# A decoder layer with retrieved experts: transposes of a listed block in one run, full-width products, later factors, earlier gathers, four selection batches

## The chip, the cores and the metric

The kernel runs on one core of a Trainium2 chip. The core has a matrix engine (PE, TensorE; its weight loads are shown apart as PEld), three engines for elementwise work (DVE or VectorE, ACT or ScalarE, POOL or GpSimd), a queue engine (SP) that issues plain transfers, and 16 DMA engines. Each engine takes its instructions in the order of the program; semaphores order the engines against each other. The metric is the time on the device, in microseconds (us), as the median of several runs; lower is better.

## The reference

One layer on 256 tokens of width 2048, in float32: attention with two kinds of heads, then a feed-forward part that looks up single-neuron experts, then a gated embedding, each with a residual and a layer norm. The change lies in the feed-forward part:

```
q  = (x @ wq) as 8 heads of 256, split into halves a and b of 128
sa, sb = a @ keys0.T, b @ keys1.T            # 128 scores each
va, ia = top_k(sa, 16);  vb, ib = top_k(sb, 16)
top, sel = top_k(va[:, None] + vb[None, :], 16)   # of 256 sums
expert = (ia * 128 + ib)[sel];  gate = softmax(top)
act = gelu(u[expert] . x)                    # u: 16384 x 2048
out = sum over the 8 * 16 experts of gate * act * v[expert]
```

So each token asks for 128 of 16384 rows of u, and for the same rows of v.

## The kernel before, in words

**Tokens in groups.** The first 32 tokens (NSP) are served one by one: 32 gathers (NSLOT) of 128 rows of u, and 32 of v, each of 128 x 2048 floats; DVE multiplies and adds what they bring (`sparse_work`, L1245; `use`, L1265). The other 224 tokens are seven groups of 32. An expert that any of them wants is *listed* in one of 43 classes by the set of groups that want it: one group, a pair, a line of three, a quad of four, or the rest. Each class has a fixed capacity, and the lists are cut into 101 blocks of 128 experts (`Block`, L85; `_blocks`, L101): 42 blocks of one group, 21 of two, 14 of three, 14 of four, 10 of all seven. `U_ORDER` (L152) is the order of the blocks in the u stage: four quads, then a mixture of quads, lines and strips of pairs, then the rest, then the singles. `V_ORDER` is that of the v stage.

**The stages around the change.**

1. *Queries and selection* (L1310 to L1334). Sixteen half-head queries run on PE (`query`, L761); ACT copies them out, PE makes the scores, and ACT copies these. DVE finds the best 16 per half (`best_scores`) and, for a batch of heads, the best pairs and their indices (`best_pairs`, L792). `BATCH` (L48) says after which query which heads are taken.
2. *Counting* (`flags`, L910). For each token DVE makes two one-hot matrices, and PE sums their products by group. In every fifth batch of eight tokens ACT makes one of the two (`act_one_hot`). `classes` (L940) turns counts into class masks, `offsets` and `running` (L998) into places in the lists; all 13 calls of `running` come before the first list.
3. *The u stage* (L1522 to L1546), the main loop. Per block, POOL issues an indirect gather of 128 rows of u (`fetch_u`, five slots). The rows are needed with the model dimension on the partitions, so PE turns them, four 128x128 transposes at a time into one PSUM bank (`turn`, L1387), and ACT copies that to `uT`. Then PE multiplies (`u_products`, L1399): the 32 tokens of a group are the stationary operand, 32 columns of the array wide, and the turned rows stream through, 128 columns; up to four groups, or four parts of one group's sum, stand side by side in the array. Transposes and products of a quarter of the block alternate, four times per block. The result has tokens on the partitions, so ACT copies it (`part`), and PE turns it back and adds the parts (`u_out`, L1424; tile `ps_A`). ACT applies gelu; where the gates stand in `W` already, DVE multiplies them in at once (L1456).
4. *Side work.* Between the quarters `side(block.cost)` lets work out in small steps, `RATE` steps per microsecond of a block's cost: the further lists (`lists`), the softmax of the gates (`gates`), the places of the experts (`list_work`, `places_of`; PE sums the positions in `ps_pos`), then the weights (`place_work`, L1116: `find` on PE, `pick` on DVE, `product` and `scale` into `W`). `gathers(block.cost * GRATE)` likewise lets out the gathers of the first 32 tokens, once the lists or the gates are through. All of it is issued with `keep`, so each engine takes it in the order written: a POOL gather stands between two row fetches, a DVE sum between two steps of side work.
5. *The v stage* (from L1551) gathers the rows of v, streams them through PE against `W`, and finishes the first 32 tokens; gathers that are still owed run here (L1586). The gated embedding and the last norm follow.

**PSUM in the u stage** has eight banks: T and U two each (transposes, products), G two (lists, ranks, `ps_find`, `ps_gT`), A one, X one (`ps_pos`, then `ps_W`).

Of the kernel before, what the change touches and what calls it, by code (L numbers as in the profile page):

```python
# [10 lines left out]
F32 = mybir.dt.float32  # L11
# [36 lines left out]
BATCH = ((0, 1), (1, 1), (2, 2), (4, 2), (6, 1), (7, 1))  # L48
NGB = 3
GSCALE = 2.0 ** 15  # L50
FB = 8
FBC = 8
# [31 lines left out]

class Block:  # L85

    def __init__(self, col, pieces):
# [10 lines left out]
        self.cost = 0.44 + 0.27 * sum({"four": 4, "two": 2, "one": 1}[w] for w, _ in self.windows)  # L98
# [53 lines left out]
U_ORDER = (BLOCKS["quad"][:4] + _mix(BLOCKS["quad"][4:], BLOCKS["line"], BLOCKS["strip"])  # L152
# [8 lines left out]
RATE, GRATE, GV = 0.75, 0.12, 0.6  # L161
# [90 lines left out]
def build(tc, a, out):  # L252
# [342 lines left out]
    XF = xfp.tile([P, ND, T], F32, name="XF")  # L595
# [196 lines left out]
    def best_pairs(h0, n):  # L792
# [4 lines left out]
        cand = tkl.tile([P, 4, NCAND], F32, name="cand", tag="cand", bufs=1)  # L797
# [12 lines left out]
        s4, s2 = (tkl.tile([P, 64], U32, name=nm)[:, :nk] for nm in ("by16", "by4"))  # L810
        pF, u1 = (tkl.tile([P, 64], F32, name=nm)[:, :nk] for nm in ("pF", "u1"))
        at = [tkl.tile([P, 64, 2], F16, name=f"at{which}")[:, :nk] for which in range(2)]
# [16 lines left out]
        for which, dst in ((0, iaN), (1, ibN)):  # L829
            eq = tkl.tile([P, 64, TOPK], F16, name="eqsel", tag="eqsel", bufs=1)[:, :nk]  # L830
# [24 lines left out]
    def gates():  # L855
# [21 lines left out]
        ps = pbank(pu, "ps_gT", "G", 2)  # L877
# [32 lines left out]
    def flags(flp):  # L910
# [11 lines left out]

        for i, t0 in enumerate(range(NSP, T, FB)):
            oa, ob = (flp.tile([P, FB, P], F16, name=nm, tag=nm, bufs=3) for nm in ("oa", "ob"))
            equal(oa, io128, iaT[:, t0:t0 + FB])
            if i % 5 == 2:
                for j in range(FB):
                    act_one_hot(ob[:, j], flp, ibF[:, t0 + j:t0 + j + 1])
            else:
                equal(ob, io128, ibT[:, t0:t0 + FB])  # L930
            made.append((t0, oa, ob))
            if len(made) > 1:
                counts()
# [64 lines left out]
    def running(k0, n, tag, on_act):  # L998

        ps = pbank(pu, "ps_run", tag, 2)  # L1000
# [60 lines left out]
    def places_of(k0, n, psp):  # L1061
# [19 lines left out]
        if psp is None:  # L1081
            keep(nc.vector.tensor_tensor(posf, posf, pk[:, 0], op=ALU.add))
            return
        for j in range(n):
            keep(nc.tensor.matmul(psp, ident, pk[:, j], start=k0 + j == 0,
                                  stop=k0 + j == KR - 1))
# [5 lines left out]
    def list_work():  # L1092

        yield from lists(UPOS[id(BLOCKS["rest"][0])])
        psp = pbank(pu, "ps_pos", "X", 1)[:, :P]
        for lo, hi in ((K1, K2), (K2, K3), (K3, K4), (K4, KR)):
            for k0, n in spread(lo, hi):
                yield from places_of(k0, n, psp)
        yield
        keep(nc.vector.tensor_copy(posf, psp))  # L1100
# [6 lines left out]
        yield from places_of(KR, 1, None)  # L1107
# [8 lines left out]
    def place_work(plp):  # L1116
# [62 lines left out]
        def product(t0, ohb, hi, lo):  # L1179
            ps = pbank(pu, "ps_W", "X", 1)  # L1180
# [197 lines left out]
    rows, turned = {}, []  # L1378
# [8 lines left out]
    def turn(k):  # L1387
        i, c = divmod(k, 4)
        if i >= NB:
            return  # L1390
        ps = pbank(pu, "ps_T", "T", 2)
# [3 lines left out]
        uT = ulp.tile([P, 512], F32, name="uT", tag="uT", bufs=4)  # L1395
        keep(nc.scalar.copy(uT, ps))  # L1396
        turned.append(uT)

    def u_products(block, c, ps, uT):  # L1399
        for w, (kind, units) in enumerate(block.windows):  # L1400
            for j in range(4):
                d = 4 * c + j
                for i, u in enumerate(units):
                    q = {"four": i, "two": 2 * i + j % 2, "one": j}[kind]
                    first = d == {"four": 0, "two": j % 2, "one": j}[kind]
                    final = d == {"four": ND - 1, "two": ND - 2 + j % 2, "one": ND - 4 + j}[kind]
                    t0 = 32 * block.units[u]
                    keep(nc.tensor.matmul(  # L1408
                        ps[32 * q:32 * q + 32, w * P:(w + 1) * P], XF[:, d, t0:t0 + 32],
                        uT[:, j * P:(j + 1) * P], start=first and not w,  # L1410
                        stop=final and w == len(block.windows) - 1))
# [11 lines left out]

    def u_out(block, part):  # L1424

        A = pbank(pu, "ps_A", "A", 1)
        col = 0
        for w, (kind, units) in enumerate(block.windows):
            x = part[:, w * P:(w + 1) * P]
            n = 32 * len(units)  # L1430
            if kind == "four":
                keep(nc.tensor.transpose(A[:, col:col + n], x, ident))
            else:
                keep(nc.tensor.matmul(A[:, col:col + n], x,
                                      stack[:, 32:96] if kind == "two" else stack[:, :32],
                                      start=True, stop=True))
            col += n
# [85 lines left out]
    for _ in range(LEAD):  # L1523
        fetch_u()
# [567 lines left out]
```

## Time and profile before

| | us |
|---|---|
| median of three runs (1668.9 to 1669.56) | 1669.44 |
| the profiled execution | 1684.18 |
| its span, first to last instruction | 1682.3 |
| mean granted TensorE clock | 0.951 |
| idle PE between 629 and 1270, of 641 | 32 |
| POOL waiting for PE to free a row slot (`uf`) | 359.8 |
| ACT waiting for PE's transposes (`uT`) | 241.7 |

The rows of the page read: line of the kernel, engine, operation, out<-in with shapes, count | busy time in us, mean ns of one | idle time of the engine just before them and what ended most of it. "128*32" before a shape is the part of the array that a matmul uses, rows by columns. A float32 matmul shows as two records, a transpose as one. Durations of PE's matmuls overlap, because the engine is pipelined; the distance from one start to the next is the safer reading. In a timeline the columns are start, length, engine, line, operation, tiles and count, and in brackets the idle time before and its releaser; "issue" means that nothing that the profile shows was waited for.

### The profile page before, as it was taken

To read this page: it belongs to the slowest core of one execution; us is meant where nothing else is said; L and a number is where in the kernel's file an instruction comes from. 1 tells how busy PE (TensorE), PEld (TensorE's weight loads), DVE (VectorE), ACT (ScalarE), POOL (GpSimd) and SP (SyncE) were. 2 spreads that over 40 slices of the span, in tenths; PEclk is the share of its full clock that TensorE was granted. 3 is DMA by queue.
4 is the path that set the end of the run, shared out by engine and by line. 5 is a ranking of instruction groups with operands and counts; after the bars stand their busy time and mean duration, and the time that the engine had idled before them with its cause. 6 is when DMAs were issued, how large, how long until landed. Compare 5 with 4: busy or idle time off the path is not lost. (4 is left out here: it accounts for less than half of the span.)

```text
span 1682.3 us, 39824 instructions
## 1 busy us (share of the span) xinstructions
PE 1533.0 (91%) x16701; PEld 1099.2 (65%) x16701; DVE 885.8 (53%) x2489; ACT 674.4 (40%) x1351; POOL 418.5 (25%) x386
## 2 busy tenths in 40 slices
PE   9999999999996559999999989899999979985698
PEld 7888888878885447777776777665667312220486
DVE  5555488864678764546465555555222220022676
ACT  5587458754110535434444322255661000011452
POOL 0133023202100212233323211132343553233000
PEclk9999999999998569999999999899999999996799
DMA  8655754585440016667877746588998999889671
GB/s 288 200 162 154 237 163 147 154 307 179 158 135 1 27 52 240 232 220 260 319 281 265 267 178 211 173 310 295 375 366 319 421 420 419 345 314 421 257 266 51
DMA packets 74617, 403.27 MB, mean 240 GB/s; under 512 B 10836, under 2 KB 12916, under 8 KB 36436
## 3 DMA queue, kind: packets, MB, share of 16 engines
q0 software_dynamic: 39280, 272.11, 42.8%
q1 hardware_dynamic: 33424, 125.41, 22.4%
q10 hardware_dynamic: 1728, 3.15, 0.5%
q8 instruction: 132, 2.16, 0.5%
q14 instruction: 53, 0.43, 0.1%
HBM read 404.97 MB, written 4.45 MB: 243 GB/s over the span
## 5 line engine op out<-in xcount | busy, mean ns | idle before, releaser
L1396 ACT COPY uT<-ps_T 128x512 f32<-128x512 f32 x404 | 235.8, 587 | 254.8 <-PE ps_T L1393 241.7
L1408 PE MATMUL ps_u<-uT,XF 128*32 128x128 f32 x8064 | 316.9, 281 | 2.3 <-issue 2.1
L213 DVE TENSOR_TENSOR wl<-wf,wh 128x1024 fp32r<-128x1024 f32 (+1 forms) x199 | 212.6, 1092 | 111.0 <-ACT wh L212 109.5
L1393 PE MATMUL ps_T<-ident,uf 128*128 128x128 f32 x1616 | 261.3, 285 | 8.2 <-DMA uf<-u_rows,idx 6.4
L1408 PEld LDWEIGHTS ps_u<-uT,XF 128*32 128x32 f32 x8064 | 202.1, 110 | 76.9 <-issue 75.8
L212 ACT CAST wh<-wf 128x1024 fp32r<-128x1024 f32 (+1 forms) x199 | 172.1, 892 | 122.9 <-PE ps_v L312 34.2
L1369 POOL DMA_INDIRECT uf<-u_rows,idx x101 | 116.3, 1151 | 421.7 <-PE ps_T L1393 359.8
L1393 PEld LDWEIGHTS ps_T<-ident,uf 128*128 128x128 f32 x1616 | 176.8, 145 | 51.7 <-issue 34.7
L1564 PE MATMUL ps_v<-vf,W 128*32 128x512 f32 x1296 | 161.9, 642 | 39.0 <-DMA vf<-v_rows,idx 38.7
L291 PE MATMUL ps_qk<-X,wh 128*128 128x512 f32 x512 | 185.2, 401 | 0.0
L1564 PEld LDWEIGHTS ps_v<-vf,W 128*32 128x32 f32 x1296 | 49.3, 113 | 148.6 <-DMA vf<-v_rows,idx 78.6
L293 PE MATMUL ps_qk<-X,wl 128*128 128x256 f32 x512 | 145.7, 285 | 0.0
L1275 DVE SCALAR_TENSOR_TENSOR y<-gb,ew,y 128x2048 f32<-128x2048 f32 x31 | 72.8, 2348 | 87.1 <-DMA gb<-v_rows,eig 87.0
L303 PE MATMUL ps_q<-XF,wf 128*128 128x256 f32 x512 | 113.5, 379 | 0.0
L291 PEld LDWEIGHTS ps_qk<-X,wh 128*128 128x128 f32 x512 | 96.4, 188 | 22.0 <-issue 1.0
L1369 POOL DMA_INDIRECT vf<-v_rows,idx x73 | 76.9, 1053 | 132.1 <-PE ps_v L1564 99.2
L1456 DVE TENSOR_TENSOR W<-W,acts 128x32 f32<-128x32 f32 (+2 forms) x86 | 13.6, 188 | 171.6 <-ACT acts L1442 167.5
L303 PEld LDWEIGHTS ps_q<-XF,wf 128*128 128x128 f32 x512 | 95.9, 190 | 12.3
L293 PEld LDWEIGHTS ps_qk<-X,wl 128*128 128x128 f32 x512 | 96.3, 188 | 2.5 <-issue 1.3
L1564 PE MATMUL ps_v<-vx,W 128*32 128x512 f32 x720 | 83.1, 612 | 7.5 <-DMA vx<-v_rows,idx 6.8
L1147 DVE SCALAR_TENSOR_TENSOR junk<-io,ibF,ps_find 128x128 f16<-128x128 f16 x224 | 63.5, 344 | 38.1 <-PE ps_T L1393 20.1
L1644 ACT COPY em<-ps_emb 128x512 f32<-128x512 f32 x2 | 1.2, 585 | 196.9 <-PE ps_emb L1640 196.9
(341 smaller groups left out, 2346.6 us busy)
## 6 DMA issues: line engine op xcount, KB each, us to landing
wf<-w_qk SPq DMA_DIRECT2D x64, 512.0 KB
wf<-w_out SPq DMA_DIRECT2D x32, 512.0 KB
wf<-peer_wq SPq DMA_DIRECT2D x16, 1024.0 KB
wf<-ple_gate SPq DMA_DIRECT2D x16, 1024.0 KB
wf<-w_v SPq DMA_DIRECT2D x16, 512.0 KB
wf<-w_sv SPq DMA_DIRECT2D x15, 512.0 KB
iarow<-s_iar SPq DMA_DIRECT2D x14, 512.0 KB
x<-x SPq DMA_DIRECT2D x2, 1024.0 KB
```

The source lines that it names most:

```text
L212: self.order(nc.scalar.copy(wh, src))
L213: self.order(nc.vector.tensor_tensor(wl, src, wh.bitcast(F32), op=ALU.subtract))
L291: nc.tensor.matmul(ps, wh[:, j * P:(j + 1) * P], xt[:, dt, :], start=dt == 0, stop=False)
L293: nc.tensor.matmul(ps[:, :T], wl[:, j * P:(j + 1) * P], xt[:, dt, :T], start=False, stop=dt == ND - 1)
L303: nc.tensor.matmul(ps[:, :T - t0], wf[:, dt * P:(dt + 1) * P], xt[:, dt, t0:], start=dt == 0, stop=dt == ND - 1)
L1147: keep(nc.vector.scalar_tensor_tensor(junk, io128, ibF[:, NSP + t:NSP + t + 1], ps[:, j * P:(j + 1) * P], op0=ALU.is_equal, op1=ALU.mult, ...
L1275: keep(nc.vector.scalar_tensor_tensor(ys, g, ew[:, j:j + 1], ys, op0=ALU.mult, op1=ALU.add))
L1369: keep(nc.gpsimd.indirect_dma_start(out=dst, out_offset=None, in_=src, in_offset=bass.IndirectOffsetOnAxis(ap=idx[:, col:col + 1], axis=0) ...
L1393: keep(nc.tensor.transpose(ps[:, j * P:(j + 1) * P], rows[i][:, (4 * c + j) * P:(4 * c + j + 1) * P], ident))
L1396: keep(nc.scalar.copy(uT, ps))
L1408: keep(nc.tensor.matmul(ps[32 * q:32 * q + 32, w * P:(w + 1) * P], XF[:, d, t0:t0 + 32], uT[:, j * P:(j + 1) * P], start=first and not w, ...
L1564: keep(nc.tensor.matmul(ps[32 * j:32 * j + 32], w, vf[:, j * 512:(j + 1) * 512], start=False, stop=last))
```

## The change

- **Transposes in one run.** `turn(i, c)` turns block i+1 while block i is the current one; the four quarters follow each other (side work between them), and only then come all products of block i. `uT` holds a whole block (two buffers of 2048 columns in place of four of 512), and T has three banks.
- **Full width.** A block of three or more groups whose group numbers make a regular pattern (`_wide`: equal steps, or two equal pairs) is multiplied the other way round: the turned rows are stationary, 128 columns, and the tokens of all its groups stream through, 32 per group. The result has experts on the partitions, so gelu reads it from the product's own bank; there is no `part` copy and no second turn. That holds for 12 of 14 quads, 4 of 14 blocks of three and all ten of seven. The block costs that pace the side work change with it.
- **Factors a block later.** DVE's multiplications by the gelu go to a list (`late`) and are issued in the next block.
- **Gathers sooner.** `GRATE` goes from 0.12 to 0.18 and `RATE` from 0.75 to 0.82; the gathers start with the first block.
- **Selection in four batches** of 3, 3, 1 and 1 heads in place of 1, 1, 2, 2, 1, 1; two casts of each batch go from DVE to ACT.
- **Counting.** ACT's six one-hot batches are written ahead of DVE's, in buffers of their own, at other places (`ACT_HOT`).
- **Run sums.** Two of the 13 calls of `running` (the quads) stay ahead of the first list; the other 11 come after the first six lists, and the order has six quads first.
- **Positions** are added on DVE in place of PE. `ps_gT` goes to bank A, `ps_W` to the two banks of G.

The diff, cut to its core:

```diff
-BATCH = ((0, 1), (1, 1), (2, 2), (4, 2), (6, 1), (7, 1))
+BATCH = ((0, 3), (3, 3), (6, 1), (7, 1))
+ACT_HOT = (5, 10, 14, 19, 23, 27)
+def _wide(units):
+    n = len(units)
+    if n < 3:
+        return None
+    steps = [y - x for x, y in zip(units, units[1:])]
+    if len(set(steps)) == 1:
+        return units[0], (1, 1), (n, steps[0])
+    if n == 4 and steps[0] == steps[2]:
+        return units[0], (2, units[2] - units[0]), (2, steps[0])
+    return None
-        self.cost = 0.44 + 0.27 * sum({"four": 4, "two": 2, "one": 1}[w] for w, _ in self.windows)
+        self.wide = _wide(self.units)
+        if self.wide:
+            self.cost = 0.44 + 4 * max(0.224, 0.053 * len(self.units))
+            return
+        self.cost = 0.44 + 0.22 * sum({"four": 4, "two": 2, "one": 1}[w] for w, _ in self.windows)
-RATE, GRATE, GV = 0.75, 0.12, 0.6
+RATE, GRATE, GV = 0.82, 0.18, 0.6
...
-        keep(nc.vector.tensor_copy(TIh[:, qs], TI[:, qs]))
+        keep(nc.scalar.copy(TIh[:, qs], TI[:, qs]))
-        keep(nc.vector.tensor_copy(pF, ci))
+        keep(nc.scalar.copy(pF, ci))
...
+        early = {}
+        for k, t0 in enumerate(range(NSP, T, FB)):
+            if k in ACT_HOT:
+                early[k] = flp.tile([P, FB, P], F16, name="obA", tag="obA", bufs=3)
+                for j in range(FB):
+                    act_one_hot(early[k][:, j], flp, ibF[:, t0 + j:t0 + j + 1])
...
-        if psp is None:
+        while n > 1:
+            h = n // 2
+            keep(nc.vector.tensor_tensor(pk[:, :h], pk[:, :h], pk[:, n - h:n], op=ALU.add))
+            n -= h
...
+        yield from lists(6)
+        for i, (k0, n) in enumerate([x for r in ((K3, K4), (K2, K3), (K1, K2))
+                                     for x in spread(*r)]):
+            running(k0, n, "TU"[i % 2], i % 3 < 2)
...
-            ps = pbank(pu, "ps_W", "X", 1)
+            ps = pbank(pu, "ps_W", "G", 2)
...
-    for i, (k0, n) in enumerate([x for r in ((K4, KR), (K3, K4), (K2, K3), (K1, K2))
-                                 for x in spread(*r)]):
-        running(k0, n, "TU"[i % 2], i % 2 == 0)
+    for i, (k0, n) in enumerate(spread(K4, KR)):
+        running(k0, n, "TU"[i], i == 0)
...
+    def u_products(block, ps, uT):
+        if block.wide:
+            n = 32 * len(block.units)
+            for d in range(ND):
+                keep(nc.tensor.matmul(ps[:, :n], uT[:, d * P:(d + 1) * P],
+                                      groups_of(d, *block.wide), start=d == 0, stop=d == ND - 1))
+            return
...
-                keep(nc.vector.tensor_tensor(dst[:, :, :m], dst[:, :, :m], x, op=ALU.mult))
+                late.append((dst[:, :, :m], x))
...
-            if not gates_done and listed > 12:
+            if not gates_done and listed > 9:
...
+    for c in range(4):
+        turn(0, c)
     for i, block in enumerate(U_ORDER):
         fetch_u()
+        old = len(late)
         for c in range(4):
-            turn(4 * i + c + 2)
-            u_products(block, c, ps, turned.pop(0))
+            turn(i + 1, c)
             if c == 1 and pending:
                 u_out(*pending)
+                pending = None
             side(block.cost)
-            if lists_done or gates_done:
-                gathers(block.cost * GRATE)
+            gathers(block.cost * GRATE)
+            if c == 1:
+                weigh(len(late) - old)
+        ps = pbank(pu, "ps_u", "U", 2)
+        u_products(block, ps, turned.pop(i))
+        if block.wide:
+            u_out(block, ps)
+        else:
+            n = P * len(block.windows)
+            part = ulp.tile([P, 512], F32, name="part", tag="part", bufs=2)
+            keep(nc.scalar.copy(part[:, :n], ps[:, :n]))
+            pending = block, part
```

More of the change, by code (lines that the diff above doesn't have):

```diff
@@ L1385, in fetch_u, with turn @@
             rows[i] = rows_of(slot("uf"), a["u_rows"], i)
-    def turn(k):
-        i, c = divmod(k, 4)
+    def turn(i, c):
         if i >= NB:
             return
-        ps = pbank(pu, "ps_T", "T", 2)
+        if not c:
+            turned[i] = ulp.tile([P, D], F32, name="uT", tag="uT", bufs=2)
+        ps = pbank(pu, "ps_T", "T", 3)
         for j in range(4):
@@ L1394, in turn @@
                                      rows[i][:, (4 * c + j) * P:(4 * c + j + 1) * P], ident))
[L1395 to L1411, printed above, removed]
+        keep(nc.scalar.copy(turned[i][:, c * 512:(c + 1) * 512], ps))
@@ new lines, in u_products @@
+    def u_products(block, ps, uT):
[6 more added lines that the diff above has]
+        for c in range(4):
+            for w, (kind, units) in enumerate(block.windows):
+                for j in range(4):
+                    d = 4 * c + j
+                    for i, u in enumerate(units):
+                        q = {"four": i, "two": 2 * i + j % 2, "one": j}[kind]
+                        first = d == {"four": 0, "two": j % 2, "one": j}[kind]
+                        final = d == {"four": ND - 1, "two": ND - 2 + j % 2,
+                                      "one": ND - 4 + j}[kind]
+                        t0 = 32 * block.units[u]
+                        keep(nc.tensor.matmul(
+                            ps[32 * q:32 * q + 32, w * P:(w + 1) * P], XF[:, d, t0:t0 + 32],
+                            uT[:, d * P:(d + 1) * P], start=first and not w,
+                            stop=final and w == len(block.windows) - 1))
@@ L1422, in regular @@
             i += n
+    late = []
     def u_out(block, part):
[L1426 to L1437, printed above, removed]
+        if block.wide:
+            A, col = part, 32 * len(block.units)
+        else:
+            A = pbank(pu, "ps_A", "A", 1)
+            col = 0
+            for w, (kind, units) in enumerate(block.windows):
+                x = part[:, w * P:(w + 1) * P]
+                n = 32 * len(units)
+                if kind == "four":
+                    keep(nc.tensor.transpose(A[:, col:col + n], x, ident))
+                else:
+                    keep(nc.tensor.matmul(A[:, col:col + n], x,
+                                          stack[:, 32:96] if kind == "two" else stack[:, :32],
+                                          start=True, stop=True))
+                col += n
         Wc = W[:, block.col]
@@ L1522, in build, with weigh @@
     gw = []
-    for _ in range(LEAD):
+    def weigh(n):
+        while len(late) > n:
+            dst, x = late.pop(0)
+            keep(nc.vector.tensor_tensor(dst, dst, x, op=ALU.mult))
+    for _ in range(WF):
         fetch_u()
-    for k in range(2):
-        turn(k)
+    for c in range(4):
+        turn(0, c)
     pending = None
```

70 lines of the change are left out of this document (37 added, 33 removed).

## The prediction

> **What bounds the kernel now.** I read the page's span and engine shares first, then a table by stages, then single stretches of the timeline, then the waits.
>
> ```profile
> span 1682.3 us, 39824 instructions
> PE 1533.0 (91%) x16701; PEld 1099.2 (65%) x16701; DVE 885.8 (53%) x2489; ACT 674.4 (40%) x1351; POOL 418.5 (25%) x386
> ...
> L1408 PE MATMUL ps_u<-uT,XF 128*32 128x128 f32 x8064 | 316.9, 281 | 2.3 <-issue 2.1
> ...
> L1393 PE MATMUL ps_T<-ident,uf 128*128 128x128 f32 x1616 | 261.3, 285 | 8.2 <-DMA uf<-u_rows,idx 6.4
> ...
> L303 PE MATMUL ps_q<-XF,wf 128*128 128x256 f32 x512 | 113.5, 379 | 0.0
> ```
>
> TensorE leads. Where is it full? The table by stages (columns: stretch, length, busy time of PE, PEld, DVE, ACT, POOL, granted clock, DMA share, GB/s):
>
> ```profile
> 414.00:534.00 120.00, 119.48 (x592) 105.73 (x590) 86.62 (x427) 15.60 (x40) 16.83 (x27) 1.00 0.33 112
> 534.00:557.00 23.00, 1.43 (x5) 0.68 (x4) 20.44 (x103) 1.21 (x4) 1.64 (x3) 0.53 0.02 3
> ...
> 629.00:1000.00 371.00, 357.61 (x6855) 272.39 (x6857) 197.66 (x777) 158.72 (x362) 101.28 (x85) 0.99 0.71 254
> 1000.00:1092.00 92.00, 81.09 (x1824) 67.34 (x1817) 51.57 (x202) 25.62 (x70) 13.84 (x14) 0.93 0.54 186
> 1092.00:1180.00 88.00, 83.01 (x1115) 53.92 (x1112) 48.77 (x176) 52.17 (x119) 25.44 (x25) 1.00 0.85 305
> 1180.00:1270.00 90.00, 87.49 (x1118) 55.73 (x1114) 22.53 (x36) 57.77 (x130) 36.89 (x33) 1.00 0.95 365
> ...
> 1300.00:1400.00 100.00, 87.22 (x754) 30.40 (x750) 25.87 (x11) 0.00 (x0) 55.05 (x41) 0.95 1.01 420
> ```
>
> The u stage (629 to 1270, 641 us, 101 blocks) has PE busy for 609 us, DVE for 321 and ACT for 294; DMA has room until its end. So the u stage is worth what PE's instruction stream is worth. From 534 to 557 DVE alone works, and from 1300 to 1400 DMA is full at 420 GB/s.
>
> What fills PE there? Two stretches of its timeline, and the weight loads of the first (idle time before in brackets):
>
> ```profile
> 705.46 0.66 PE L1393 MATMUL ps_T<-ident,uf 128*128 128x128 f32 x4
> 706.04 1.08 PE L1408 MATMUL ps_u<-uT,XF 128*32 128x128 f32 x32
> 707.05 1.16 PE L1085 MATMUL ps_pos<-pk,ident 128*128 128x128 f32 x8
> ...
> 709.03 0.65 PE L1408 MATMUL ps_u<-uT,XF 128*32 128x128 f32 x16
> 709.60 0.66 PE L1393 MATMUL ps_T<-ident,uf 128*128 128x128 f32 x4
> ...
> 710.93 1.06 PE L1085 MATMUL ps_pos<-pk,ident 128*128 128x128 f32 x8
> 711.82 0.38 PE L1066 MATMUL ps_rank<-I,upto 128*128 128x512 f16 x1
> ```
>
> ```profile
> 705.46 0.42 PEld L1393 LDWEIGHTS ps_T<-ident,uf 128*128 128x128 f32 x4 [0.20 <-issue]
> 706.04 0.81 PEld L1408 LDWEIGHTS ps_u<-uT,XF 128*32 128x32 f32 x32 [0.17 <-issue]
> ...
> 708.05 0.43 PEld L1068 LDWEIGHTS <-cs 128*128 128x128 f16 x4
> 708.43 0.42 PEld L1393 LDWEIGHTS ps_T<-ident,uf 128*128 128x128 f32 x4
> ```
>
> I take starts, since ends are modelled. Four transposes to the next products: 0.58 (705.46 to 706.04), of which the loads fill 0.42. Products of 32 records take 1.01, of 16 records 0.57 (709.03 to 709.60): (1.01 - 0.57)/16 = 0.0275 per record, and 0.57 - 16 x 0.0275 = 0.13 that belongs to no record. So each change between 128*128 and 128*32 costs 0.16 one way, 0.13 the other, and the load row shows it as an idle 0.17 or 0.20 with no wait behind it. Between two 128*128 kinds (708.43) there is none. A block pays this four times: 4 x 0.29 = 1.16 us.
>
> **The change: the u stage.** From the block table in the code: 101 blocks, 252 groups; 26 become wide (12 of four groups, 4 of three, 10 of seven), 75 stay narrow (42 of one group, 21 of two, 10 of three, 2 of four).
>
> - *Transposes in one run.* A narrow block changes shape once each way: 0.87 saved, x 75 = 65. A wide block never does: 1.16 x 26 = 30.
> - *Wide products.* 16 matmuls of two records each. 8 full records with 128 columns take 0.89 (710.93 to 711.82), 0.111 each: 32 x 0.111 = 3.55 us. Four narrow groups are 4 x 32 x 0.0275 = 3.52: nothing gained. Seven groups stream 224 columns: L303 gives 113.5/512 = 0.222 for 256, so 0.194 x 32 = 6.2 against 6.16: nothing. Three groups lie between 0.083 (streaming 96 of 128 columns) and 0.111 (a load of 128 columns that does not shrink); I take 0.111, the nearest row: 3.55 against 2.64, +0.9 x 4 = +4. The Trainium skill, "TensorE: Matmul & The Clock Gate", section LDWEIGHTS, says that load time goes by the columns loaded, 128/1.2 = 107 ns, which speaks against full width for three groups; by it the term is the +4, by streaming alone it is 0.
> - *No second turn.* Wide blocks drop the copy into part (ACT, hidden) and the A matmuls: two records of L1434 take 0.25 (1212.14 to 1212.39, below) and a transpose 0.42/4 = 0.1, so a block of seven drops 3 x 0.25 + 0.1 = 0.85, of three 0.75, of four 0.1: 9 + 3 + 1 = 13.
> - *Positions summed on DVE.* 84 full records (L1085) x 0.111 = 9 leave PE; some 30 additions, each no dearer than the picks below (0.34), go to DVE, which has 320 us idle.
> - *Run sums later.* 11 of the 13 calls of running move into the stage: 72 short records, between 0.055 (128 columns at half of 0.111) and 0.11: +4.
>
> Sum: -65 - 30 + 4 - 13 - 9 + 4 = -109; 641 becomes 532.
>
> ```profile
> 1212.14 0.41 PE L1434 MATMUL ps_A<-stack,part 128*128 128x32 f32 x2
> 1212.39 0.64 PE L1393 MATMUL ps_T<-ident,uf 128*128 128x128 f32 x4
> ```
>
> ```profile
> L1396 ACT COPY uT<-ps_T 128x512 f32<-128x512 f32 x404 | 235.8, 587 | 254.8 <-PE ps_T L1393 241.7
> ...
> L1275 DVE SCALAR_TENSOR_TENSOR y<-gb,ew,y 128x2048 f32<-128x2048 f32 x31 | 72.8, 2348 | 87.1 <-DMA gb<-v_rows,eig 87.0
> ...
> L1147 DVE SCALAR_TENSOR_TENSOR junk<-io,ibF,ps_find 128x128 f16<-128x128 f16 x224 | 63.5, 344 | 38.1 <-PE ps_T L1393 20.1
> ```
>
> And from the list of waits (who waited for whom: us in total, times, longest):
>
> ```profile
> DVE W L1456 <- ACT acts L1442: 167.5, 51, 9.7
> ...
> DVE y L1275 <- DMA gb<-v_rows,eig: 87.0, 13, 14.0
> ...
> PE ps_W L1183 <- DVE W L1190: 16.6, 15, 3.0
> ```
>
> What comes late next? *Factors later* removes DVE's 167.5 us of waiting for gelu; DVE is not the bound, so by itself it is worth 0, but it makes room for the 32 second gathers' additions. *ps_W into G's two banks* removes up to 16.6 of PE waiting; but one ps_W stays open while two ps_find are made, three tiles on two banks, so ps_find can wait for its pick (4 x 0.34 us), 0 to 1 us in each of 56: -17 to +40, taken as 0. *Gathers sooner* puts all 64 beside the u blocks. On POOL each stands between two row fetches (POOL: 177 us busy of 641 in the four rows), on DVE each costs 2.35 us. With 128 x 2048 x 4 bytes = 1.05 MB for each, the stage moves (101 + 64) x 1.05 + 14 x 0.5 + four early v rows = 184 MB: 346 GB/s over 532 us. That fits in 420, but not everywhere. Side work on PE is 609 - 404 x (0.58 + 0.13) - 8064 x 0.0275 - 270 x 0.125 = 66 us, 0.65 a block, of which 9 leave: say 0.5. A block of one group then takes 4 x 0.42 + 0.29 + 32 x 0.0275 + 0.25 + 0.5 = 3.6 us, and with 4 x 0.66 x 0.18 = 0.475 gathers brings 1.55 MB: 430 GB/s. The row 1180:1270 gives 365/0.95 = 384 at full share, so 4.0 us. By the costs in the code 52 gathers are out when these blocks begin; the other 12 last for 25 blocks: 25 x 0.4 = +10. u stage: 542, **-99**.
>
> **The other stages.** Selection:
>
> ```profile
> 509.10 0.29 DVE L754 MAX8 TV<-S 128x8 f32<-128x128 f32 x1 [3.00 <-ACT S L773]
> ...
> 512.26 0.62 DVE L802 TENSOR_TENSOR cand<-TV 128x192 f32<-128x192 f32 x2
> ...
> 526.03 0.28 DVE L754 MAX8 TV<-S 128x8 f32<-128x128 f32 x1
> ...
> 532.31 0.41 DVE L802 TENSOR_TENSOR cand<-TV 128x96 f32<-128x96 f32 x2
> ...
> 541.00 0.28 DVE L754 MAX8 TV<-S 128x8 f32<-128x128 f32 x1
> ```
>
> A batch of two heads takes 13.8 (512.26 to 526.03), of one 8.7 (532.31 to 541.00): 3.6 fixed, 5.1 per head. Six batches to four save 7.2 of DVE time, but before 509 DVE had to wait for scores anyway (3.00 in the row). What stands behind the last wait grows from 2 heads to 3: +5.1, less about 1 for six casts that go to ACT (each smaller than the 0.28 of MAX8): **+4**. The casts make ACT wait for DVE's list; behind it stand the copies qT and S, and PE's ps_k waits for those: up to 9 us, hidden as PE has ended at 534 and DVE at 556; if it isn't, PE's end moves by that.
>
> Counting and the start of the u stage (ACT's, then DVE's timeline):
>
> ```profile
> 565.46 0.31 ACT L894 ACTIVATE ob<-dist 128x128 f16<-128x128 f16 x1 [1.67 <-PE ps_cnt L920]
> ```
>
> ```profile
> 602.91 0.56 DVE L946 TENSOR_SCALAR f<-ps_cnt 128x384 f16<-128x384 f32 x1 [4.12 <-PE ps_cnt L920]
> ...
> 614.53 0.56 DVE L1009 CAST run<-ps_run 128x384 f16<-128x384 f32 x1 [1.29 <-PE ps_run L1004]
> ...
> 619.84 0.56 DVE L1009 CAST run<-ps_run 128x384 f16<-128x384 f32 x1 [0.45 <-PE ps_run L1004]
> ```
>
> *One-hots of ACT ahead.* ACT is what ends the count: DVE is through 4.12 before it. Five times (565.46 is the first) ACT waited some 1.67 for a buffer that PE held. With three buffers of its own and the first used at the sixth batch it runs through: 5 x 1.67 = **-8**. *Two run sums ahead of the first list, not 13:* the stretch from 614.5 to 619.8 goes: **-5**. *v stage:* of 1300:1400 PE lost 12.8 us while DMA also brought gathers; those are gone: **-12**. The blocks of one group at its end stay bound by DMA.
>
> Total -99 + 4 - 8 - 5 - 12 = -120. The profiled execution took 1684.2 us (span 1682.3); 1564 is its forecast. The median of the three runs is 1669.4, 14.8 lower; the same 120 off gives **1549 us**.
>
> **Rivals.** (1) *DMA takes over the u stage.* If it keeps the 305 GB/s of 1092:1180, 184 MB take 603 us: -38 in place of -99, 1610. For it: 0.85 share at 305 there, more gathers now; against: 420 at 1300:1400. The Trainium skill, "DMA: Bandwidth & Descriptors", Specifications, gives a core about 358 GB/s of HBM; by that the stage would be 514 at least, so PE still decides; the 420 exceeds it, and the measurement holds. (2) *ACT paces the run.* Four copies of 0.587 are 2.35 us against 1.68 of transposes; if each run waited for them, 0.67 x 101 = 68 is lost: 1617. Against: three banks, and products of the block before stand between the runs; ACT is busy 294 of 641. (3) *The 0.29 belongs to each four transposes, not to the change of shape* (the change does not do what it says): the 95 stay, 1644. Against: 708.43 starts without a gap. (4) *Slower.* DVE is in order: if each of 64 gathers makes it wait 6.7 us (87.0/13) in the u stage, DVE needs 321 + 32 x 2.35 + 429 = 825 us, with PE's ps_find and ps_W behind it: 283 more than 542, 1832. It decides from a mean wait of some 4.2 us on, where DVE needs 542 + 120 = 662. Against: the 32 first gathers were used in the u stage with no such wait in the list; 87.0 was beside full DMA.
>
> **How the numbers follow.** Forecast 0.68, rivals 0.14, 0.08, 0.05, 0.05. Range 1512 to 1622: below by the ps_W gain and queued rows (-27) and a little more, above to rivals 1 and 2; left out are 3, 4 and tails, under 0.2. A change under 0.2% cannot be told from none: faster 0.94, same 0.01, slower 0.05.
>
> **What would show it.** PE's runs of 16 transposes without gaps; 32 wide records in some 3.55 us; blocks of one group at 3.5 to 4 us; count end 8 earlier; last selection 4 later relative to the last score; no gathers after the u stage. A PE idle share over 15% in the u stage with DMA share near 1 would mean rival 1; with DVE's row waiting on gathers, rival 4.

## The result and the profile after

The changed kernel takes 1586.51 us (median of four runs, 1582.58 to 1587.39), the kernel before 1669.38 beside it: ratio 0.9499, interval 0.9483 to 0.9516, 83 us less. The forecast was 1549 in a range of 1512 to 1622. The profiled execution took 1586.15, its span 1584.4. Two executions of the runs below, one of e8 (3581.1 us) and one of e11 (1663.14), took much longer than the others of the same kernel and are left out of the times given.

The page after, the rows that answer to those of before (for L1430, the full-width products, there was no row before):

```profile
span 1584.4 us, 32495 instructions
PE 1417.8 (89%) x13183; PEld 1165.9 (74%) x13183; DVE 884.5 (56%) x2464; ACT 647.7 (41%) x1340; POOL 435.4 (27%) x386
...
L1424 ACT COPY uT<-ps_T 128x512 f32<-128x512 f32 x404 | 222.2, 596 | 80.3 <-PE ps_T L1422 77.8
L1422 PE MATMUL ps_T<-ident,uf 128*128 128x128 f32 x1616 | 228.6, 281 | 21.2 <-DMA uf<-u_rows,idx 20.0
...
L1430 PE MATMUL ps_u<-XF,uT 128*128 128x128 f32 (+2 forms) x832 | 139.2, 330 | 0.0
...
L1443 PE MATMUL ps_u<-uT,XF 128*32 128x128 f32 x3904 | 124.2, 277 | 1.5 <-issue 1.4
...
L1304 DVE SCALAR_TENSOR_TENSOR y<-gb,ew,y 128x2048 f32<-128x2048 f32 x31 | 72.7, 2346 | 17.1 <-DMA gb<-v_rows,eig 17.0
```

PE's transposes cost 33 us less than before (261.3), its products 53 (139.2 + 124.2 against 316.9), and ACT's wait for transposes fell from 241.7 to 77.8. Did the run of transposes come out as meant? PE's timeline, a block of two groups and then a quad:

```profile
762.75 1.96 PE L1443 MATMUL ps_u<-uT,XF 128*32 128x128 f32 x64
764.63 0.66 PE L1422 MATMUL ps_T<-ident,uf 128*128 128x128 f32 x4
765.13 0.33 PE L1049 MATMUL ps_rows<-run,mark 128*128 128x129 f16 x3
765.30 0.60 PE L1422 MATMUL ps_T<-ident,uf 128*128 128x128 f32 x4
...
766.97 3.74 PE L1430 MATMUL ps_u<-XF,uT 128*128 128x128 f32 x32
770.54 0.60 PE L1422 MATMUL ps_T<-ident,uf 128*128 128x128 f32 x4
```

Yes: from start to start 64 narrow records take 1.88 us (the prediction's 0.13 + 64 x 0.0275 is 1.89), 32 wide ones 3.57 (3.55). PE's part fits the prediction here.

So where is the time that was expected and did not come? The stages, from landmarks in the two traces (the ends of the last ps_q, last ps_iT and last ps_cnt, the first uf, the first ps_T, the ends of the last ps_u and of the last x<-ps_v):

| stretch | before | after | change | predicted |
|---|---|---|---|---|
| end of queries to last index transpose | 24.0 | 31.3 | +7.3 | +4 |
| counting | 45.9 | 37.7 | -8.2 | -8 |
| to the first row fetch | 19.8 | 14.5 | -5.3 | -5 |
| u stage | 640.6 | 570.8 | -69.8 | -99 |
| v stage | 305.7 | 284.9 | -20.8 | -12 |

The rest moves by -1.0, so the spans differ by 97.9. The u stage is the miss. Its blocks come in three kinds, in this order: 49 quads, triples and pairs mixed, ten of seven groups, 42 of one group. The table by stretches (length, busy time of PE, PEld, DVE, ACT, POOL, granted clock, DMA share, GB/s), before and then after:

```profile
628.00:960.00 332.00, 323.78 (x6033) 244.07 (x6034) 176.34 (x700) 147.65 (x328) 95.47 (x79) 0.99 0.73 262
960.00:1091.00 131.00, 114.46 (x2633) 95.57 (x2630) 72.05 (x270) 35.81 (x98) 20.60 (x21) 0.95 0.54 186
1091.00:1269.00 178.00, 171.22 (x2238) 110.06 (x2236) 72.14 (x217) 110.56 (x251) 62.28 (x58) 1.00 0.90 336
```

```profile
620.00:898.00 278.00, 267.65 (x4445) 249.88 (x4446) 211.10 (x766) 138.07 (x321) 116.40 (x91) 0.98 0.92 350
898.00:1035.00 137.00, 105.17 (x718) 98.29 (x717) 78.78 (x245) 27.85 (x91) 31.91 (x23) 0.86 0.57 205
1035.00:1191.00 156.00, 140.06 (x2293) 123.63 (x2292) 76.67 (x242) 101.96 (x250) 74.56 (x57) 0.96 0.96 379
```

The mixed blocks gave 54 us, the singles 22. The ten blocks of seven got 6 us *longer*: PE is busy for only 105 of 137 us there, DMA runs at 0.57, DVE at 79 of 137, and the clock is at 0.86. No engine is full. The side work there is a chain: PE makes a `ps_find`, DVE picks the values out of it (`junk`) and makes one-hots of them (`ohb`), PE multiplies these into `ps_W`, and DVE scales that into `W`. One block of seven shows why it is slow. DVE's timeline, then PE's:

```profile
954.95 0.39 DVE L1576 TENSOR_TENSOR W<-W,acts 128x32 f32<-128x32 f32 x3 [7.02 <-ACT acts L1492]
...
956.87 2.34 DVE L1304 SCALAR_TENSOR_TENSOR y<-gb,ew,y 128x2048 f32<-128x2048 f32 x1
...
960.02 0.68 DVE L800 TENSOR_TENSOR ohb<-io,row 128x1024 f16<-128x1024 f16 x1
```

```profile
946.57 7.96 PE L1430 MATMUL ps_u<-XF,uT 128*128 128x224 f32 x32
954.36 0.60 PE L1422 MATMUL ps_T<-ident,uf 128*128 128x128 f32 x4
954.80 0.39 PE L1168 MATMUL ps_find<-map,oht 128*128 128x128 f16 x4
955.02 1.51 PE L1422 MATMUL ps_T<-ident,uf 128*128 128x128 f32 x12
960.75 0.21 PE L1212 MATMUL ps_W<-hi,ohb 128*128 128x42 f16 x1 [4.22 <-DVE ohb L800]
...
961.32 7.53 PE L1430 MATMUL ps_u<-XF,uT 128*128 128x224 f32 x32
968.69 1.04 PE L1422 MATMUL ps_T<-ident,uf 128*128 128x128 f32 x8
```

While PE multiplies for 7.8 us (946.57 to 954.36), DVE waits 7.02 of them. Then PE has 1.7 us of transposes and needs DVE's one-hots, which DVE begins only now, behind the picks and a gather's sum of 2.34: PE waits 4.22. The two engines take turns. And the wait costs twice: the clock after it, in a table like the one above,

```profile
946.50:950.00 3.50, 3.50 (x14) 3.18 (x12) 1.16 (x8) 0.00 (x0) 0.83 (x1) 0.54 0.70 176
...
957.00:961.00 4.00, 0.25 (x7) 0.25 (x8) 3.96 (x6) 0.29 (x1) 1.76 (x2) 0.93 0.58 190
961.00:965.00 4.00, 4.00 (x28) 3.78 (x25) 1.59 (x5) 0.00 (x0) 0.00 (x0) 0.65 0.82 332
965.00:968.50 3.50, 3.50 (x20) 3.50 (x19) 0.00 (x0) 0.00 (x0) 0.00 (x0) 1.00 0.02 7
```

is 0.65 for 4 us, then 1.00. (The first row is the block before, whose products come behind waits of 0.81 and 2.51.) Without a wait ahead such products take 6.05 from start to start (989.62 to 995.67); here it is 7.37.

### The profile page after: what moved, and what is told of

Read it like the earlier page. It is cut to its first block, busy times and chain, and to the rows that moved or that the text cites. A ratio compares the mean times of both kernels' runs of the same rounds, so it can differ in the third digit from the quotient of the medians.

```text
span 1584.4 us, 32495 instructions
## 1 busy us (share of the span) xinstructions
PE 1417.8 (89%) x13183; PEld 1165.9 (74%) x13183; DVE 884.5 (56%) x2464; ACT 647.7 (41%) x1340; POOL 435.4 (27%) x386
## 5 line engine op out<-in xcount | busy, mean ns | idle before, releaser
L1424 ACT COPY uT<-ps_T 128x512 f32<-128x512 f32 x404 | 222.2, 596 | 80.3 <-PE ps_T L1422 77.8
L1422 PE MATMUL ps_T<-ident,uf 128*128 128x128 f32 x1616 | 228.6, 281 | 21.2 <-DMA uf<-u_rows,idx 20.0
L1397 POOL DMA_INDIRECT uf<-u_rows,idx x101 | 137.3, 1360 | 335.2 <-PE ps_T L1422 259.2
L1422 PEld LDWEIGHTS ps_T<-ident,uf 128*128 128x128 f32 x1616 | 182.4, 146 | 37.2 <-issue 20.5
L1627 PE MATMUL ps_v<-vf,W 128*32 128x512 f32 x1296 | 162.0, 642 | 31.3 <-DMA vf<-v_rows,idx 31.1
L1627 PEld LDWEIGHTS ps_v<-vf,W 128*32 128x32 f32 x1296 | 78.6, 113 | 110.7 <-issue 59.3
L1681 DVE BATCH_NORM_STATS2 st<-ps_v 128x6 f32<-128x512 f32 x8 | 5.6, 699 | 243.7 <-PE ps_v L1717 182.9
L1430 PE MATMUL ps_u<-XF,uT 128*128 128x128 f32 (+2 forms) x832 | 139.2, 330 | 0.0
L1430 PEld LDWEIGHTS ps_u<-XF,uT 128*128 128x128 f32 x832 | 132.0, 209 | 2.8
L1443 PE MATMUL ps_u<-uT,XF 128*32 128x128 f32 x3904 | 124.2, 277 | 1.5 <-issue 1.4
L1443 PEld LDWEIGHTS ps_u<-uT,XF 128*32 128x32 f32 x3904 | 103.3, 111 | 13.4 <-issue 11.6
```

What stands on the lines that cost most here:

```text
L1397: keep(nc.gpsimd.indirect_dma_start(out=dst, out_offset=None, in_=src, in_offset=bass.IndirectOffsetOnAxis(ap=idx[:, col:col + 1], axis=0) ...
L1422: keep(nc.tensor.transpose(ps[:, j * P:(j + 1) * P], rows[i][:, (4 * c + j) * P:(4 * c + j + 1) * P], ident))
L1424: keep(nc.scalar.copy(turned[i][:, c * 512:(c + 1) * 512], ps))
L1430: keep(nc.tensor.matmul(ps[:, :n], uT[:, d * P:(d + 1) * P], groups_of(d, *block.wide), start=d == 0, stop=d == ND - 1))
L1443: keep(nc.tensor.matmul(ps[32 * q:32 * q + 32, w * P:(w + 1) * P], XF[:, d, t0:t0 + 32], uT[:, d * P:(d + 1) * P], start=first and not w, ...
L1627: keep(nc.tensor.matmul(ps[32 * j:32 * j + 32], w, vf[:, j * 512:(j + 1) * 512], start=False, stop=last))
```

## The experiments

My first theory was that DVE, which takes its work in order, stands at the gelu factors of a block of seven whose products PE has not ended. The rivals: the two banks of G for three kinds of side tiles; the loads; the wide products themselves. The variants below are the changed kernel with one edit each; `e0` is the kernel before. The runs fell on three chips. On two of them the kernel before takes 1670.94 and 1669.93 us, on the third, where e0, e1, e6 and e3 ran, 1681.64. So ratios to the kernel before on the same chip are given throughout.

**The kernel before, again.**

> The kernel before, profiled a second time. Its first profile was 14.7 us above the median of its runs, the changed kernel's profile is level with its median (1586.2 against 1586.5). If the first profile was a slow execution, this one comes near 1669 and shows which stage was long by some 15 us (the stretch 629 to 1270 of the first, 641 us, would be nearer 626, and the gain of the u stage in the medians some 55 and not 70). If a profile of this kernel always adds that much, it is near 1684 again with the same stages.

One execution: 1682.33 us, span 1680.5, u stage 637.7. It repeats the profile before (1684.18), which therefore looks like an execution on such a chip; the 14.7 us between that profile and its median would then lie between chips.

**Factors one block later still** (e1): a wide block's factors are issued in the next block only after those of the block before.

```diff
-    pending = None
+    pending, fresh = None, 0
...
-        old = len(late)
+        old = len(late) - fresh
...
+        fresh = 0
         if block.wide:
+            fresh = -len(late)
             u_out(block, ps)
+            fresh += len(late)
```

> The changed kernel, with the factors of a full-width block issued a whole block later than now (at the second quarter of the block after next). Theory: DVE stands in order behind these factors, which wait for the gelu of products that PE has not ended (94 us of DVE idle in the u stage, 41 of them in the blocks of seven), so PE then finds its one-hots and picks not made (32 us idle there) and loses clock (some 17 us). Then most of the 94 goes, except DVE's scale that waits for W (18 us), and the time falls by 15 to 35 us, to 1552 to 1571. Rival, two banks for three tiles: the waits of ps_find stay, the time falls by under 10. Rival, loads bind: no change within 5 us.

Ratio 0.9565 (0.9539 to 0.9591), 1610.03 us: no gain. The ten blocks of seven took 133 us, 4 less than in the changed kernel, with PE idle for 29.7:

```profile
920.00:1053.00 133.00, 103.31 (x734) 96.90 (x731) 78.01 (x245) 28.10 (x92) 31.86 (x23) 0.88 0.57 207
```

The longest waits of that stretch, changed kernel and then this one:

```profile
DVE W L1576 <- ACT acts L1492: 31.9, 6, 7.0
...
PE ps_W L1212 <- DVE ohb L800: 19.5, 8, 4.2
```

```profile
DVE junk L1176 <- PE ps_find L1168: 34.4, 10, 7.0
...
PE ps_W L1212 <- DVE ohb L800: 17.7, 8, 4.2
```

DVE's wait for the gelu is gone, and in its place it waits as long for the next ps_find, which stands in PE's list behind the same products. So the first theory falls: the factors are where DVE happens to stand. The second theory, then: DVE stands because PE has no side work among the products. Side steps are bunched between the transposes; a PE run of 6 us leaves DVE with nothing, and 1.7 us of transposes cannot cover DVE's steps.

**Side work between the quarters of the products, in all wide blocks** (e6).

```diff
+                if d % 4 == 3:
+                    side(block.cost)
+                    gathers(block.cost * GRATE)
...
-            side(block.cost)
-            gathers(block.cost * GRATE)
+            if not block.wide:
+                side(block.cost)
+                gathers(block.cost * GRATE)
```

> The changed kernel, with the side work and the gathers of a full-width block issued between the quarters of its products and no longer between its transposes. Theory: the side work has then some 1.5 us of products as cover after each quarter, DVE meets no gelu that is still to come, PE's waits for ps_W and ps_find (37 us) fall under 12 and the half clock in the blocks of seven goes: 30 to 45 us less, 1541 to 1557. Rival, two banks: ps_find waits as before, at most 20 less. Rival, the wide products themselves are slow: no gain, since they still take some 7.5 us for seven groups.

Ratio 0.9414 (0.9387 to 0.9441), 1585.14 us, 25 less than e1 on the same chip. The blocks of seven fell to 99 us, but the mixed blocks took 310 in place of 278. Of these 32 us, 22 are not in the edit: e1 has them too (300), and e1 gives PE the same instructions in the same order as the changed kernel up to the v stage. The other 10 may be the edit's, in the blocks of three and four groups; that stays open. The narrow products of the u stage, changed kernel and then e1:

```profile
L1443 PE MATMUL ps_u<-uT,XF 128*32 128x128 f32 x3904 | 123.4, 276 | 0.9 <-issue 0.9
```

```profile
L1443 PE MATMUL ps_u<-uT,XF 128*32 128x128 f32 x3904 | 137.4, 276 | 10.9 <-issue 10.3
```

(The first row is of the second execution of the changed kernel, e8 below.) In 22 of the 75 unbroken runs of such records, in e1 and in e6, PE stops in the middle, for 0.2 to 0.7 us at a time, and waits for nothing that the trace shows. From first to last record the 75 runs take 127.9 us in e1, 130.0 in e6, and 105.1 in the changed kernel.

**Narrow products for all blocks** (e3): `self.wide = None`.

> The changed kernel without full-width blocks: all blocks go by 32 columns, transposes still in one run. By the prediction's terms, full width saves one change of shape both ways and the second turn: 26 x 0.29 + 13 - 4 = 17 us; without it the time would be 1603. Theory: its unbroken products also bring the waits (32 us idle and 17 of half clock in the blocks of seven, against some 6 to 22 without), so that the two about cancel: 1575 to 1595. Rival, loads bind: 1587 within 5.

Ratio 0.9705 (0.9676 to 0.9734), 1634.24 us: 24.2 more than e1 on the same chip. Of that, 16.7 are the same stops of PE, now in 41 runs (35.4 us, 18.7 in e1, counting what each pause has over 0.1). The other 7.5 are roughly what full width is worth here; by the prediction's terms for wide blocks beside runs in one piece (26 x 0.29 - 4 + 13) it is 17. Both expectations missed, by some 40 us or more, of which the stops are 35. The stretch of the ten blocks of seven, and PE's longest waits there:

```profile
944.00:1080.00 136.00, 110.51 (x2706) 99.76 (x2702) 80.21 (x255) 35.97 (x108) 33.85 (x23) 0.95 0.57 208
```

```profile
PE ps_find L1168 <- DVE junk L1176: 11.3, 7, 2.7
PE ps_u L1443 <- issue: 6.0, 12, 1.9
PE ps_W L1212 <- DVE ohb L800: 5.8, 4, 2.0
```

So narrow products in one run don't shorten the stretch (133 in e1). PE waits some 18 us for DVE's picks and one-hots there, against 30 in e1 and 14.5 in the kernel before. Long runs and full width are thus not separated by this variant: the waits are fewer without full width, and why stays open.

**The changed kernel again** (e8).

> The changed kernel itself, unaltered. In the three variants timed so far the 75 unbroken runs of 128*32 products in the u stage took 127.9 and 130.0 us from first to last record (3904 records), against 105.1 in the profile of the changed kernel, though the first of them issues the same TensorE instructions in the same order up to the v stage; 22 runs hold gaps of 0.2 to 0.7 us in which TensorE waits for nothing that the trace shows. Theory A (the gaps belong to the chip or to where the program was loaded, and come back whenever 64 to 192 TensorE instructions of 32 columns follow one another): the same kernel now shows them, some 128 us in those runs, and takes 1600 to 1612. Rival B (the gaps came with the edits): no gaps, 105 us, 1582 to 1590.

1586.38 us, ratio 0.9493 (0.9447 to 0.9539), the runs of narrow products 103.7 us, two with a stop. Theory A as I put it has failed: the stops do not come back wherever many narrow records follow one another. Theory B, that the edits bring them, falls too: five variants below with the same long runs (e9, e4, e2, e5, e13), on the other two chips, have them in one to three runs. And e0, the kernel before with no edit, has them on that chip: 21 stops in 19 of its 403 shorter runs, 5.1 us, all in runs of 24 to 56 records, so shorter runs are not free of them. (The first profile of the kernel before has 21 as well, 5.5 us.) The stops are shown on one chip, in all four kernels that ran there. What PE lacks there stays open; the changed kernel itself was not run on that chip.

**Side work between the quarters, in blocks of seven alone** (e9).

```diff
+                if d % 4 == 3 and len(block.units) > 4:
+                    side(block.cost)
+                    gathers(block.cost * GRATE)
...
-            side(block.cost)
-            gathers(block.cost * GRATE)
+            if len(block.units) < 5 or not block.wide:
+                side(block.cost)
+                gathers(block.cost * GRATE)
```

> Only in the ten blocks of seven groups, the listing, factors and gathers are issued after each quarter of the block's products instead of between its transposes; all other blocks as in the changed kernel. Theory (in those blocks VectorE, in order, stands at factors whose products are not done, TensorE then waits over 3 us for one-hots and picks, and its clock halves): the stretch of the ten blocks falls from 137 us to about 100, as in the variant with all wide blocks cut, the clock there stays over 0.97, and the total falls by 25 to 38 us against the changed kernel on the same chip. Rival (the side work is only moved, and the blocks of one group, which wait on loads, take the gain back): the stretch falls, but the total by less than 8.

1548.19 us, ratio 0.9269 (0.9231 to 0.9307): 38 less than the changed kernel on the same chip. Its u stage by the same three stretches:

```profile
621.00:899.00 278.00, 267.80 (x4443) 249.48 (x4444) 210.98 (x766) 137.91 (x321) 116.70 (x91) 0.98 0.92 350
899.00:999.00 100.00, 91.96 (x706) 87.39 (x703) 77.25 (x241) 28.31 (x96) 25.53 (x24) 0.97 0.78 282
999.00:1154.00 155.00, 140.71 (x2306) 123.83 (x2306) 78.62 (x247) 101.44 (x246) 72.39 (x57) 0.96 0.96 383
```

Only the middle row differs from the changed kernel's: 100 for 137. PE's idle time there goes from 32 to 8, and its busy time from 105 to 92, as the clock goes from 0.86 to 0.97; so 24 us were waiting and 13 were work at a lower clock. Nothing later takes it back. The second theory stands in what it says of the remedy: nothing but the place of the steps was changed.

**The narrow blocks' products in quarters again** (e10): u_products is called for quarter c behind `turn(i + 1, c)` where the block is narrow.

> The first part of the change undone for the narrow blocks alone: a listed block's products go in four pieces again, each behind the four transposes of the next block's quarter; wide blocks keep their run. Theory of the prediction (each change between 128*128 and 128*32 costs 0.16 one way and 0.13 the other, six more of them in each narrow block): 75 blocks x 3 x 0.29 = 65 us longer than the changed kernel where that has no gaps, and some 45 where it has, since pieces of 16 to 48 records leave no gaps. Rival (the changes of shape were hidden, and what the run saved was waiting for the copies): less than 15 either way.

1623.13 us, ratio 0.9713 (0.9677 to 0.975): 37 more. The singles of this variant:

```profile
1133.82 0.66 PE L1422 MATMUL ps_T<-ident,uf 128*128 128x128 f32 x4
1134.41 0.42 PE L1443 MATMUL ps_u<-uT,XF 128*32 128x128 f32 x8
1134.76 0.41 PE L1484 MATMUL ps_A<-stack,part 128*128 128x32 f32 x2
```

```profile
1057.00:1230.00 173.00, 171.37 (x2291) 110.93 (x2288) 77.57 (x242) 111.66 (x251) 71.09 (x57) 1.00 0.90 342
```

The singles of e8, and PE's longest wait in them:

```profile
1036.00:1191.00 155.00, 137.90 (x2281) 121.82 (x2283) 76.86 (x242) 101.86 (x250) 76.52 (x57) 0.97 0.96 382
```

```profile
PE ps_T L1422 <- DMA uf<-u_rows,idx: 12.9, 6, 9.3
```

The price of a change of shape is as predicted: four transposes take 0.59 to the start of narrow products, against 0.44 with a full-array matmul behind them (954.36 to 954.80 above), so 0.15; and 0.35 for eight records of 0.0275, 0.13. But PE is full here (171 of 173), where in e8 it is idle for 17 of 155, 13 of these waiting for rows of u, at a DMA share of 0.96. Of the 42 x 0.87 = 37 us that the run should save in the singles, 18 are left (173 against 155); in the mixed blocks 19 of 33 x 0.87 = 29 (296 against 277).

**Selection as before** (e4): six batches, both casts on DVE.

> Only the selection as before: six batches, and the casts of its positions on VectorE. The stretch from the last query product to the last index transpose was 24.0 us before and 31.3 with the change, where the prediction had 4 more. Theory (the two batches of three make the last one end later, and the casts on ScalarE wait in its queue): 24 to 25 us again, and the total 6 to 8 lower, about 0.4%. Rival (later stages give it back, since the counting and the first loads then start earlier but wait for the same data): the stretch falls, the total does not.

1576.98 us, ratio 0.9441 (0.9404 to 0.9479); on the same chip its runs (1574.92 to 1579.75) lie clear of the changed kernel's (1585.97 to 1586.55). The stretch is 24.0 us again, counting stays at 37.7, the u stage is 2.6 shorter. The end of selection, from last query to last index, changed kernel and this one:

```profile
530.50:561.80 31.30, 2.03 (x8) 1.20 (x8) 27.72 (x140) 2.44 (x9) 2.17 (x4) 0.55 0.02 4
```

```profile
531.60:555.60 24.00, 2.04 (x9) 1.20 (x8) 21.33 (x109) 1.47 (x5) 1.58 (x3) 0.56 0.02 3
```

6.4 of the 7.3 us are DVE's own work that now lies behind the last query, 0.9 waiting. The total is 9 lower, so this part of the change is a loss.

**A bank of its own for ps_W** (e2), and two in place of three for the transposes.

> The W products get a PSUM bank of their own (the transposes keep two banks of three), so that three side tiles no longer share two banks. Theory (in the blocks of seven PE waits because the side steps stand close together between the transposes, with nothing of PE's own between a find and the next: a third bank lengthens the chain by one tile only): the stretch of the ten blocks stays at 125 to 138 us, the total within 8 us of the changed kernel's 1586. Rival (the two banks are the cause, which the prediction priced at -17 to +40 and took as 0): the stretch falls to about 105 and the total by 25 to 35.

1578.91 us, ratio 0.9456 (0.9418 to 0.9495). The blocks of seven took 120 us, between the two expectations, and the u stage 9 less. The bank replaces the wait, it does not end it: in that stretch ps_W now waits 19.7 us for DVE's scaling of the tile before. So the banks are a part of it, some 17 of the 37 us that e9 finds. The mixed blocks and the singles are 5 us longer each, with one bank less for the transposes; how the total moves is within the intervals.

**Gathers as before** (e5): `GRATE = 0.12`, and none before the lists or gates are done.

> Only the gathers as before: a rate of 0.12 in place of 0.18, and none until the listing or the gates are done, so that some stand beside the v stage again. Theory of the prediction (with all 64 in the u stage the blocks of one group pay 10 for the transfers and the v stage gains 12): the u stage 5 to 12 shorter, the v stage 8 to 21 longer, the total -4 to +15. Rival (the gathers hold up POOL's row fetches in the u stage): the u stage over 15 shorter, the total lower by more than 8.

1589.47 us, ratio 0.9508 (0.9473 to 0.9543): no difference to the changed kernel. It is not quite the old order: block costs are lower now, so 46 of the 64 gathers start in the u stage, against 51 in the kernel before and all 64 in the changed kernel. Both sets of numbers missed: the u stage was 538.0 us, 32 less than e8, and the v stage 322.3, 37 more. The gathers cost about the same wherever they are; 20 of the 32 are in the blocks of seven (118 us, 138 in e8), where DVE has 9 gathers' sums to make and not 14, at some 2.3 us each.

**The two gains together** (e11: e9 and e4), **and the first v rows four blocks later** (e13: `i >= NB - LEAD - 1`).

> The two variants that were faster on their own, together: side work between the quarters of the products in the blocks of seven, and the selection as before. If their gains are apart in the program they add: 38 and 9 below the changed kernel, 1536 to 1543. If the earlier start of the u stage only moves the program into the same loads: 1544 to 1550.

> The variant before, with the first loads of v rows issued four blocks later in the u loop. In the profile of the changed kernel four of them go out at 1129 to 1134 ahead of eleven rows of u, and TensorE then stands 8.9 us for a row of u at 1143.8. Theory (those loads take that place, and nothing needs them yet): the u stage 5 to 9 shorter, the v stage at most 3 longer. Rival (the transfers are at their limit there, and what u gains v loses): the total within 3 us of the variant before.

e11: ratio 0.9221 (0.9184 to 0.9259); the runs compared lie between 1537.28 and 1543.77. The gains add, within the intervals: 0.9269 x 0.9441/0.9493 = 0.9218. e13: 0.9216 (0.9184 to 0.9248), the same; there PE still waits 11.9 us for rows of u in the singles (10.8 in e9), which speaks for the transfers themselves and not for their order. Both beat the changed kernel by some 45 us.

## Why the prediction was right, and where it was not

The likeliest case came true, 37 us above its number and within its range.

- *Right, term by term:* the price of a change of shape, 0.13 to 0.16 us (e10), and none between two 128*128 shapes, so rival 3 is out; wide products at 3.57 and 6.05 us for 3.55 and 6.2; counting -8.2 for -8; start of the u stage -5.3 for -5; blocks of one group 156/42 = 3.7 us, in the predicted 3.6 to 4.0. The copies on ACT (rival 2) held up PE by less than 1 us.
- *Transposes in one run: -65 for the narrow blocks.* Mis-sized: e10 measures 38 in the u stage (608.4 against 570.3). The saving per change is real, but PE was counted as the only bound; with shorter blocks something else is late in part of them. In the singles PE's busy time falls by 33 of the 37 us, but its idle time grows by 16 (2 in e10, 17 in e8), most of it waiting for rows of u, which is rival 1 in part. In the mixed blocks 10 are missing, and what takes them wasn't isolated.
- *"Factors later ... by itself worth 0", "ps_W into G's two banks ... taken as 0".* Here a step is missing rather than mis-sized. The prediction asked which engine is full, and none is. It did not ask what PE has to do between a find and the one-hots that follow it. With products and transposes in turns there was always some of both; the change puts all side steps between the transposes. In the mixed blocks, whose side work is in part another, PE waits 2.8 us for picks and one-hots, in the blocks of seven 31.8 (14.5 before). By the prediction's own rates a block of seven is 1.68 + 6.2 + 0.5 = 8.4 us, ten are 84; measured 137, and 100 with the steps spread out (e9).
- *Half the clock.* Not in the sum at all: 13 us in the blocks of seven. The trace's own record of the clock has eight spells of 0.50 there, each 3.41 or 6.83 us long, 37.5 us in all, and their starts lie whole multiples of 3.41 us apart. The Trainium skill, "TensorE: Matmul & The Clock Gate", Part 1: The HAM clock gate, says that the clock falls to half after an idle window of some 3.4 us, that windows run freely, and that it takes a busy one to come back. The trace agrees on the windows, but they need not be idle throughout. In the u stage of the changed kernel, at full clock, half clock followed each window of 3.41 us in which PE was busy for 1.46 us or less, and none in which it was busy for 1.99 or more. So waits of 0.81 and 2.51 with work between them were enough once (clock 0.54 in the next 3.5 us).
- *Selection +4.* Mis-sized: +7.3. I counted one head more behind DVE's last wait; DVE's work behind the last query grew by 6.4.
- *v stage -12 and gathers +10.* Both mis-sized, and in opposite ways: e5 moves 32 us out of the u stage and 37 into the v stage. The sum of the two, -2, was about right (-5).
- *The scale.* The sum was made against a profile 14.7 us above the median. The changed kernel's profile is at its median, so the spans differ by 97.9 and the times by 83. The kernel before differs by 11 us between chips. In which stages was not seen, since its profiles are both of the longer kind; 5 us of each are the stops of PE described under e8. The v stage of the changed kernel is as short on the slower chip (283.6 in e1, 284.9 in the changed kernel's profile), so its gain is not one of chips.

Where the sum fell short is seen by laying out its own terms by stretch. The mixed blocks should have come to 279 us (332 - 29 - 19 for the changes of shape, - 4 for the second turn, - 9 for the positions, + 4 + 4). The ten blocks of seven should have come to 111 (131 - 12 - 8), the singles to 151 (178 - 37 + 10). They took 278, 137 and 156. So of the 29 us that the u stage is short, 26 lie in the blocks of seven. In the mixed blocks the forecast is met although the run of transposes gave 10 less there, so something that the sum does not name gave as much (some 3 of it may be the stops of PE in the profile before); that part is luck. With selection 3 short and the v stage 9 over, the spans are 22 short of 120; the other 15 of the 37 us are the scale.

The experiments measure more than that: e9 finds 38 in the blocks of seven, e10 27 too few in the narrow ones, e4 9 in selection, and e2 and e5 shorten the same waits as e9 by other means. These overlap, and are not meant to add up.

## What to carry to other kernels

When long runs of one engine are made by pushing other steps out of them, look at what the pushed-out steps need of each other: here a chain from PE to DVE and back wanted PE work between its links, and the long unbroken run left both engines waiting in turn. If the busy times of a stretch show no engine full, suspect the order of issue: moving the wait (e1) or adding a buffer (e2) helped less than spreading the steps (e9). And take a bundle apart afterwards: one of its parts cost 9 us, another was worth nothing.

## What was not expected of the hardware

- A change between 128*128 and 128*32 matmuls costs PE 0.13 to 0.16 us each way, with the wait put down to nothing; 225 pairs fewer were worth 37 us.
- PE's clock was halved for whole windows of 3.41 us behind windows in which PE had worked for as much as 1.46 us.
- On one of three chips PE stopped in the middle of unbroken runs of narrow records, mostly of 64 and more, for 0.2 to 0.7 us at a time (twice longer in e3, up to 2.2), 18 to 35 us in all; in e1 with the same instructions in the same order as on a chip where it hardly did.
- The kernel before takes 1681.64 us on that chip and 1669.93 and 1670.94 on the two others, at the same mean clock of 0.95; so times of different chips are compared by ratios only.
